# Six rows of 1/rms by way of memory in place of products with the identity

## The chip, the cores and the metric

The kernel runs on one core of one Trainium2 chip. The metric is the device time of an execution in microseconds, the median of several runs.

## The reference

One layer of a bidirectional hybrid encoder over 512 tokens of width 1024, all in float32. What matters here is the RMS normalisation, which occurs six times in the part that is changed:

```
def rms_norm(x, g):
    y = xf * lax.rsqrt(jnp.mean(xf * xf, axis=-1, keepdims=True) + EPS)
    return (y * g).astype(x.dtype)

def gated_group_rmsnorm(y, z, g):           # four groups of 512 columns
    v = (y * silu(z)).reshape(bsz, s, SSD_GROUPS, d // SSD_GROUPS)
    v = v * lax.rsqrt(jnp.mean(v * v, axis=-1, keepdims=True) + EPS)
```

The layer normalises x, makes one wide input projection, runs a state space branch (SSD: a convolution, two chunked scans, a gated RMS norm in four groups, a projection) and a branch of windowed attention, merges both by sigmoid gates, projects and adds to x; then cross-attention into 256 normalised memory tokens (its queries come from rms_norm(x)), then a SwiGLU FFN (its input is rms_norm(x)), then a last rms_norm.

## The kernel before, in words

Activations lie transposed: 128 features on the partitions, 512 tokens along the free axis. Each product runs in three matmuls per 128 x 128 weight block, on a high and a low part of both operands (`mac`, L134 to L141); a projection (`proj`) has 24 of them and gathers its result in one PSUM bank. The banks have three tags: "mm" (three banks, for projections), "sa" (two) and "sb" (three, for small things).

A normalisation's factor 1/rms depends on the token alone, so the kernel applies it after the projection: the projection runs on x times the gain, and its result is multiplied by a row that holds 1/rms of each token, the same on all partitions. Three steps make that row. A sum of squares by token is gathered while x is produced. `rms_stat` (L149 to L167) sums it over the partitions by matmuls against a column of ones, which leaves a token on each partition and a column for each of the four chunks of 128 tokens, and takes the power -0.5 on GpSimd (POOL, L161) with one refining step on VectorE (L163 to L166); its result r is 128 x 4. `rms_row` (L176) then turns r into the row: `rms_bank` (L169) multiplies, for each chunk, a column of r spread over 128 columns with the identity (L172), which puts the row on all partitions of an "sb" bank, and ScalarE copies it to SBUF (L178).

Rows made so, apart from those of the first stage and of the end: `vrow` for each of the four scan groups (`group_row`), `row1` in the cross-attention (`xa_row`) and `row2` in the FFN (`ff_row`). Their readers:

- `group_out` (L636): eight results of an out projection are multiplied by `vrow` on VectorE (L644 in the first group, L647 in the others) and added to the branch's sum on POOL (L648). Each result holds an "mm" bank until its product with the row.
- `xq_out` (L943): VectorE multiplies a q result by `row1` (L949), ScalarE and VectorE split it into a high and a low part (L950, L951); the scores (`xattend`, L966) of a head need two such tiles.
- `ff_act` (L1044): VectorE multiplies a gate result by `row2` (L1048), ScalarE takes SiLU, POOL multiplies by the row again (L1050), VectorE by the up result (L1052).

The program is a list of steps, which names the weights that each step needs; weights are loaded two steps ahead by the sync engine's queue and split by ScalarE (L129) and VectorE (L130). Up to the step `cutat`, which lies behind the last scan group, the steps stand in a block whose order on each engine a planner works out from its own estimates of durations (`tc.block(schedule_with_timeline_sim=True)`); the later steps are ordered by the default planning. In either case each engine runs its instructions in the order planned. In the scan, POOL weights the inputs (L495), masks the decay rows (L537) and adds the two directions (L550); VectorE multiplies that sum (L555) before TensorE uses it (L565). In the steps list of a group, the statistics and the row of the group before are woven into the first half of the scan; for the last group they stand at the end of the scan, followed by `group_out(3)`. The gates of the branch (`early_gate`, L653 to L659) are further projections near the end of the scan whose results ScalarE empties.

Of the kernel before, what the change touches and what calls it, by code (L numbers as in the profile page):

```python
# [9 lines left out]
F32 = mybir.dt.float32  # L10
# [5 lines left out]
P = 128  # L16
D = 1024
S = 512
KT = D // P
NCH = S // P  # L20
# [52 lines left out]
def bidir_hybrid_layer(ctx: ExitStack, tc: tile.TileContext, io, dbg=None):  # L73
    nc = tc.nc
# [9 lines left out]
    dram = ctx.enter_context(tc.tile_pool(name="dram", bufs=1, space=bass.MemoryType.DRAM))  # L84
# [9 lines left out]
    def bank(tag):  # L94
        return ps.tile([P, 512], F32, tag=tag, name=tag, bufs={"mm": 3, "sa": 2, "sb": 3}[tag])
# [73 lines left out]
    def rms_bank(r, nchunk):  # L169
        rb = bank("sb")  # L170
        for c in range(nchunk):
            nc.tensor.matmul(rb[:, c * P:(c + 1) * P], r[:, c:c + 1].broadcast_to([P, P]), ident,  # L172
                             start=True, stop=True)
        return rb

    def rms_row(pool, r, nchunk, tag, bufs=1):  # L176
        row = pool.tile([P, S], F32, tag=tag, name=tag, bufs=bufs)[:, :nchunk * P]
        nc.scalar.copy(row, rms_bank(r, nchunk)[:, :nchunk * P])  # L178
        return row

    def add_square(pool, acc, t, first, n, eng, tag="sq", bufs=1):
# [15 lines left out]
    st = {}  # L197
# [56 lines left out]
    def mem_row():  # L254
        st["mrow"] = rms_row(st["sp"], st["mr"], 2, "sq", 1)
# [52 lines left out]
    def x_row():  # L308
        st["xrow"] = rms_row(st["sp"], st["xr1"], NCH, "vrow")
# [356 lines left out]
        st["vr"] = rms_stat(st["sp"], st["vsq"], NCH, S, 4.0 * EPS)  # L666

    def group_row():
        st["vrow"] = rms_row(st["sp"], st["vr"], NCH, "vrow")

    add(ssd_open)
    first, last = group_in(0)
# [2 lines left out]
    for g in range(G):  # L675
        z, (more, turn) = group_z(g), group_in(g + 1) if g + 1 < G else ([], [])
        scan1, scan2 = group_scan(g)
        out = group_out(g - 1) if g else kv[KV1:]
        early = [(early_gate(m), (full(io["w_in"][G_GS + m]),)) for m in range(4)] if g == G - 1 else []
        kinds = {"m": list(more), "z": z[ZP:], "o": list(out), "e": early,  # L680
                 "r": [(group_rms, ())] if g else [], "w": [(group_row, ())] if g else []}

        def take(order):
            return [kinds[c].pop(0) for c in order if kinds[c]]

        one = take(ONE if g < G - 1 else ONE + "e")
        if g == 0:
            one += take("o" * len(kinds["o"]))
        two = take(TWO if g < G - 1 else LAST)
        steps += z[:ZP] + last  # L690
        steps += weave(scan1, one)
        steps += weave(scan2, two)
        last = turn
    add(group_rms)
    add(group_row)
    steps += group_out(G - 1)
    add(apply_early)
# [235 lines left out]
        st["xr2"] = rms_stat(st["xa"], st["acc1"], NCH, D, EPS)  # L933

    def xa_row():
        st["row1"] = rms_row(st["xa"], st["xr2"], NCH, "row1")

    def xq_step(m):
        def f(w):
# [72 lines left out]
    add(xa_rms)  # L1012
    steps += xq[1:2]
    add(xa_row)
    for h in range(4):
        if h < 3:
# [17 lines left out]
        st["xr3"] = rms_stat(st["ff"], st["acc2"], NCH, D, EPS)  # L1034

    def ff_row():
        st["row2"] = rms_row(st["ff"], st["xr3"], NCH, "row2")

    def ff_in(i):
        def f(w):  # L1040
# [72 lines left out]
    for j in range(FKT):  # L1113
        add(ff_in(2 * j), full(io["w_fi"][2 * j]))
        if j == 0:
            add(ff_rms)
        add(ff_in(2 * j + 1), full(io["w_fi"][2 * j + 1]))
        if j == 0:
            add(ff_row)
        add(ff_act(j))  # L1120
# [120 lines left out]
```

## Time and profile before

| | |
|---|---|
| median of 3 runs | 1302.97 us (1302.38 to 1303.30) |
| profiled execution | 1303.36 us, its span 1301.6 us |
| TensorE (PE) busy | 1253.2 us, 96% of the span |
| VectorE (DVE) busy | 773.0 us, 59% |
| ScalarE (ACT) busy | 565.5 us, 43% |
| GpSimd (POOL) busy | 290.7 us, 22% |
| granted TensorE clock | 0.991 of 2.4 GHz |

Times in the rows are microseconds from the span's start. An engine's busy time adds up its instructions; the bracket behind an instruction says how long its engine had been idle before it and which instruction ended the idle time.

### The profile page before, as it was taken

The page shows a single profiled execution, that of the slowest core. Times are in us where ns is not written, and L with a number is a line of the kernel's source. Part 1 is how long each engine was busy: PE and PEld are TensorE (multiplying, and loading weights), DVE is VectorE, ACT ScalarE, POOL GpSimd, SP SyncE. Part 2 cuts the span into 40 slices and gives each one's busy share as a digit, 9 for nine tenths or more (in the row PEclk, how much of TensorE's full clock was granted, in tenths as well). Part 3 has the DMA queues.
Part 4 walks back from the last instruction along what each step waited for, and adds up shares of the span by engine and source line. Part 5 has one row for each costly group of instructions (what it writes and reads, how often), then busy time and mean ns, then how long its engine had stood idle before and what let it go on. Part 6 is the DMA issues. An engine that isn't in the chain of part 4 may idle for free.

```text
span 1301.6 us, 16248 instructions
## 1 busy us (share of the span) xinstructions
PE 1253.2 (96%) x6076; PEld 1011.6 (78%) x6076; DVE 773.0 (59%) x1235; ACT 565.5 (43%) x1062; POOL 290.7 (22%) x250
## 2 busy tenths in 40 slices
PE   7998899999989999999999999999999999999996
PEld 5776588778678688877667888887888888888886
DVE  6785896687777865678873445665444444432323
ACT  6557645365455232358783234444332222222220
POOL 2004722442571733111000002001111111110001
PEclk9999899999999999999999999999999999999998
DMA  7446553454354232321114333322322223233331
GB/s 252 153 138 179 160 166 122 130 157 135 108 152 131 85 120 69 120 98 33 49 34 145 97 99 104 123 65 65 97 94 97 96 94 95 97 97 96 92 98 65
DMA packets 49614, 143.48 MB, mean 110 GB/s; under 512 B 5120, under 2 KB 8576, under 8 KB 49536
## 3 DMA queue, kind: packets, MB, share of 16 engines
q1 hardware_dynamic: 47536, 138.58, 34.5%
q0 software_dynamic: 704, 2.10, 0.4%
q10 hardware_dynamic: 1296, 1.77, 0.4%
q8 instruction: 48, 0.79, 0.3%
q14 instruction: 30, 0.25, 0.1%
HBM read 137.97 MB, written 4.46 MB: 109 GB/s over the span
## 4 chain that ended last, share of the span: by engine, by line
PE 59%; issue 5%; DVE 2%; ACT 2%; POOL 1%; DMA 0%; DVEq 0%; ACTq 0%; POOLq 0%
PE mm L139 18%; PE mm L141 18%; PE mm L140 18%; PE sb L823 1%; PE sb L810 1%; PE sb L997 1%; PE sa L966 1%; POOL rsw L722 1%; PE sa L782 1%; ACT rsw L721 0%; ACT whi L129 0%; PE sa L784 0%; ACT sm L795 0%; PE sb L154 0%; PE sb L172 0%
## 5 line engine op out<-in xcount | busy, mean ns | idle before, releaser
L129 ACT CAST whi<-raw 128x1024 fp32r<-128x1024 f32 (+2 forms) x192 | 199.0, 1036 | 467.6 <-PE mm L140 390.7
L139 PE MATMUL mm<-hh,whi 128*128 128x512 f32 x968 | 382.5, 396 | 5.6 <-DVE cvu L414 2.2
L141 PE MATMUL mm<-hh,wlo 128*128 128x512 f32 x968 | 380.5, 393 | 0.9 <-DVE wlo L130 0.9
L140 PE MATMUL mm<-hl,whi 128*128 128x512 f32 x968 | 380.0, 393 | 0.0
L130 DVE TENSOR_TENSOR wlo<-raw,whi 128x1024 fp32r<-128x1024 f32 (+2 forms) x202 | 250.3, 1239 | 153.8 <-ACT whi L129 144.1
L139 PEld LDWEIGHTS mm<-hh,whi 128*128 128x128 f32 x968 | 182.7, 189 | 47.0 <-issue 5.7
L141 PEld LDWEIGHTS mm<-hh,wlo 128*128 128x128 f32 x968 | 182.6, 189 | 40.2 <-issue 1.8
L140 PEld LDWEIGHTS mm<-hl,whi 128*128 128x128 f32 x968 | 182.8, 189 | 36.8 <-issue 1.0
L544 ACT ACTIVATE rt<-rt,nb 128x128 f32<-128x128 f32 x256 | 78.4, 389 | 61.7 <-POOL rt L537 61.7
L187 POOL TENSOR_TENSOR sq_acc<-sq_acc,sq 128x512 f32<-128x512 f32 x14 | 24.3, 1738 | 262.9 <-ACT sq L186 262.9
L1050 POOL TENSOR_TENSOR fa<-fa,row 128x512 f32<-128x512 f32 x22 | 39.0, 1775 | 192.4 <-ACT fa L1049 192.4
L139 PE MATMUL mm<-vh,whi 128*128 128x512 f32 (+1 forms) x192 | 71.1, 371 | 9.2 <-DVE cvu L414 5.6
L139 PE MATMUL mm<-fh,whi 128*128 128x512 f32 (+1 forms) x198 | 72.6, 367 | 0.0
L140 PE MATMUL mm<-fl,whi 128*128 128x512 f32 (+1 forms) x198 | 72.4, 365 | 0.0
L141 PE MATMUL mm<-fh,wlo 128*128 128x512 f32 (+1 forms) x198 | 72.3, 365 | 0.0
L414 DVE SCALAR_TENSOR_TENSOR cvu<-mm,hcw,cvu 128x510 f32<-128x510 f32 (+1 forms) x96 | 71.1, 743 | 1.3
L141 PE MATMUL mm<-vh,wlo 128*128 128x512 f32 (+1 forms) x192 | 70.5, 367 | 0.0
L140 PE MATMUL mm<-vl,whi 128*128 128x512 f32 (+1 forms) x192 | 68.4, 356 | 0.0
L537 POOL TENSOR_SCALAR_AFFINE_SELECT rt<-rt 128x512 f32<-128x512 f32 x64 | 48.0, 776 | 57.4 <-DMA rt<-adr 55.5
L1052 DVE TENSOR_TENSOR ft<-fa,mm 128x512 f32<-128x512 f32 x22 | 15.1, 688 | 72.9 <-PE mm L141 70.7
L550 POOL TENSOR_TENSOR mt<-rt 128x512 f32<-128x512 f32 x32 | 46.1, 1454 | 19.8 <-PE sa L565 19.8
L139 PEld LDWEIGHTS mm<-vh,whi 128*128 128x128 f32 x192 | 36.6, 190 | 17.8 <-issue 7.3
(230 smaller groups left out, 1941.0 us busy)
## 6 DMA issues: line engine op xcount, KB each, us to landing
raw<-in_w_in SPq DMA_DIRECT2D x69, 512.0 KB, 3.5
raw<-in_w_fi SPq DMA_DIRECT2D x44, 512.0 KB, 3.5
rt<-adr SPq DMA_DIRECT2D x32, 512.0 KB, 5.5
ear<-edr SPq DMA_DIRECT2D x32, 256.0 KB, 4.4
raw<-in_w_bs SPq DMA_DIRECT2D x16, 512.0 KB, 3.5
raw<-in_w_fo SPq DMA_DIRECT2D x16, 512.0 KB, 3.5
raw<-in_w_xk SPq DMA_DIRECT2D x8, 512.0 KB, 3.5
raw<-in_w_ba SPq DMA_DIRECT2D x8, 512.0 KB, 3.5
```

What stands on the lines that cost most here:

```text
L129: nc.scalar.copy(hi[:, t], raw[:, t])
L130: (nc.gpsimd if i in LO_POOL else nc.vector).tensor_tensor(lo[:, t], raw[:, t], hi[:, t].bitcast(F32), op=ALU.subtract)
L139: nc.tensor.matmul(acc, wh, xh[:, k0 + k], start=first and k == 0, stop=False)
L140: nc.tensor.matmul(acc, wh, xl[:, k0 + k], start=False, stop=False)
L141: nc.tensor.matmul(acc, wl, xh[:, k0 + k], start=False, stop=last and k == nk - 1)
L187: eng.tensor_tensor(acc, acc, sq, op=ALU.add)
L414: nc.vector.scalar_tensor_tensor(u[:, b], acc[:, a], w5[j], u[:, b], op0=ALU.mult, op1=ALU.add)
L537: nc.gpsimd.affine_select(out=rt[:, d].rearrange("p (c l) -> p c l", c=NCH), in_=rt[:, d].rearrange("p (c l) -> p c l", c=NCH), pattern=[[ ...
L544: nc.scalar.activation(r, r, AF.Exp, bias=st["nb"][:, c, e0:e0 + 1])
L550: nc.gpsimd.tensor_tensor(mt, st["rt", g, h][:, 0], st["rt", g, h][:, 1], op=ALU.add)
L1050: nc.gpsimd.tensor_tensor(a, a, st["row2"], op=ALU.mult)
L1052: nc.vector.tensor_tensor(t, a, st["fp", 2 * j + 1], op=ALU.mult)
```

## The change

The six rows named above go another way. r (128 x 4, a token on each partition) is written to a small tensor in memory in the order of the tokens, by a DMA that POOL issues; a second DMA, also issued by POOL, reads these 512 numbers back as a row for each of the 128 partitions. The products with the identity and the copy by ScalarE go. The first stage's rows and the last normalisation keep the old way.

```diff
     def rms_row(pool, r, nchunk, tag, bufs=1):
         row = pool.tile([P, S], F32, tag=tag, name=tag, bufs=bufs)[:, :nchunk * P]
         nc.scalar.copy(row, rms_bank(r, nchunk)[:, :nchunk * P])
+        return row
+
+
+    def rms_sent(pool, r, tag):
+        rdr = dram.tile([1, S], F32, tag="rdr", name="rdr", bufs=2)
+        nc.gpsimd.dma_start(rdr.rearrange("o (c p) -> p (o c)", p=P), r)
+        row = pool.tile([P, S], F32, tag=tag, name=tag, bufs=1)
+        nc.gpsimd.dma_start(row, rdr.broadcast_to([P, S]))
         return row
...
     def group_row():
-        st["vrow"] = rms_row(st["sp"], st["vr"], NCH, "vrow")
+        st["vrow"] = rms_sent(st["sp"], st["vr"], "vrow")
...
     def xa_row():
-        st["row1"] = rms_row(st["xa"], st["xr2"], NCH, "row1")
+        st["row1"] = rms_sent(st["xa"], st["xr2"], "row1")
...
     def ff_row():
-        st["row2"] = rms_row(st["ff"], st["xr3"], NCH, "row2")
+        st["row2"] = rms_sent(st["ff"], st["xr3"], "row2")
```

## Rows read from the trace of the kernel before

**Rows 1.** Busy time of each engine by stage: us, then each engine, clock, DMA.

```profile
core 0: us, PE busy (x) PEld busy (x) DVE busy (x) ACT busy (x) POOL busy (x), PEclk, DMA share, GB/s
...
395.00:495.00 100.00, 97.76 (x495) 77.26 (x494) 73.34 (x91) 36.63 (x62) 39.62 (x30) 1.00 0.37 111
495.00:538.00 43.00, 41.49 (x190) 34.08 (x189) 24.21 (x33) 7.39 (x10) 12.88 (x9) 1.00 0.28 91
...
926.00:1162.00 236.00, 236.00 (x1051) 195.64 (x1050) 96.89 (x115) 71.53 (x90) 38.28 (x22) 1.00 0.30 96
```

**Rows 2.** The chain that ended last, around the last group's row: start, us, what.

```profile
505.27 0.91 PE sb L172 x8
506.20 0.59 ACT vrow L178
506.82 0.70 DVE cvt L647
507.57 0.50 PE mm L139
```

**Rows 3.** Timeline, last scan group: r's last step, and the matmul that waited.

```profile
504.13 0.16 DVE L166 SCALAR_TENSOR_TENSOR rms_r<-rms_t,rms_r 128x4 f32<-128x4 f32 x1
...
507.57 0.50 PE L139 MATMUL mm<-vh,whi 128*128 128x512 f32 x1 [1.40 <-DVE cvt L647]
```

**Rows 4.** Timeline, cross-attention, from r to the first scores and the turn.

```profile
818.83 0.16 DVE L166 SCALAR_TENSOR_TENSOR rms_r<-rms_t,rms_r 128x4 f32<-128x4 f32 x1
...
821.02 0.59 ACT L178 COPY row<-sb 128x512 f32<-128x512 f32 x1
...
825.60 0.69 DVE L951 TENSOR_TENSOR ql<-qf,qh 128x512 fp32r<-128x512 f32 x1 [0.69 <-ACT qh L950]
...
826.30 0.28 PE L966 MATMUL sa<-kvh,qh 128*128 128x256 f32 x1
...
834.73 1.03 PE L986 MATMUL sb<-cst,pe 128*128 128x128 f32 x8
```

**Rows 5.** Timeline, FFN: r, its row, and the starts of two products.

```profile
934.17 0.16 DVE L166 SCALAR_TENSOR_TENSOR rms_r<-rms_t,rms_r 128x4 f32<-128x4 f32 x1
...
938.84 0.59 ACT L178 COPY row<-sb 128x512 f32<-128x512 f32 x1
...
944.12 0.39 PE L139 MATMUL mm<-hh,whi 128*128 128x512 f32 x1
...
949.56 0.39 PE L139 MATMUL mm<-hh,whi 128*128 128x512 f32 x1
```

**Rows 6.** Timeline, first and third scan group: r, POOL's work, the row.

```profile
228.24 0.16 DVE L166 SCALAR_TENSOR_TENSOR rms_r<-rms_t,rms_r 128x4 f32<-128x4 f32 x1
...
231.30 1.04 POOL L495 TENSOR_TENSOR xw<-xk,wt 128x512 f32<-128x512 f32 x1 [0.82 <-PE sb L503]
...
238.33 0.59 ACT L178 COPY vrow<-sb 128x512 f32<-128x512 f32 x1 [1.04 <-PE sb L172]
...
238.74 2.52 POOL L550 TENSOR_TENSOR mt<-rt 128x512 f32<-128x512 f32 x2 [6.39 <-PE sa L565]
...
426.06 0.16 DVE L166 SCALAR_TENSOR_TENSOR rms_r<-rms_t,rms_r 128x4 f32<-128x4 f32 x1
...
434.55 0.59 ACT L178 COPY vrow<-sb 128x512 f32<-128x512 f32 x1 [3.31 <-PE sb L172]
```

**Rows 7.** DMA issues: queue, count, KB each, median us from issue to landing.

```profile
rt<-adr SPq DMA_DIRECT2D x32, 512.0 KB, 5.5
ear<-edr SPq DMA_DIRECT2D x32, 256.0 KB, 4.4
...
out_t<-x ACTq DMA_DIRECT2D x8, 128.0 KB, 1.9
```

**Rows 8.** POOL's stores of 128 KB: ns min/median/max on POOL, us to landing.

```profile
L262 POOL DMA_DIRECT2D kdr<-xw x8: 539/557/598, 48.2 to 172.3; - x8
...
DMA to landing us min/median/max: 2.2/2.6/9.5
```

## The prediction

> **What bounds the kernel now.** I read the busy time by stage first: TensorE (PE) is busy 98% in the stretch that holds the third scan group's row, 96% in the one that holds the last group's and 100% in the FFN's first half, with the clock granted in full [rows 1]. No other engine is near that. So what takes an instruction off PE is a gain where PE never waits, and what makes PE wait is a loss of the same size, with no later idle time to win it back from: the stages behind are as full.
>
> Next I read the chain that ended last around the last group's row. It runs through the very thing that is changed: the products with the identity (0.91 us), the copy by ScalarE, VectorE's product with the row (L647), and only then the next matmul [rows 2]. PE stands there because a result tile can be emptied only once the row is known, and all three "mm" banks hold such results. The timeline gives the times: r, the four columns of 1/rms, is ready at 504.13 + 0.16 = 504.29, the row at 506.20 + 0.59 = 506.79, and PE goes on at 507.57, released by L647 [rows 2, 3]. From r to row it is 2.5 us, and from row to the next matmul 0.78.
>
> I then looked at the five other rows for the same two times. In xa, r is ready at 818.99, the row at 821.61, and the first score product, which needs two q tiles made from the row, starts at 826.30 [rows 4]. In ff, r is ready at 934.33 and the row at 939.43; the product that needs a freed bank starts at 944.12, and such a product takes 949.56 - 944.12 = 5.44 us [rows 5]. In the first scan group r is ready at 228.40 and the row at 238.92; the second group repeats this 100 us later; in the third it is 426.22 and 435.14 [rows 6]. So the time that each row may take before it is later than today is 10.5, 10.5, 8.9, 2.5, 2.6 and 5.1 us.
>
> **What the change removes.** Six times four products (eight matmul instructions): 0.9 us of PE each, 5.4 in all, by the 0.91 of the chain [rows 2]. Six copies of 0.59 us on ScalarE, which is no bound anywhere, and one "sb" bank for their length: nothing.
>
> **What it adds: the trip.** Each row becomes a store by token, issued on POOL's queue, and a load of 2 KB to each of 128 partitions, also on POOL's queue, which can't be issued before the store has landed. Call T the time from r to the row in SBUF; it is serial. No row shows a store of 512 pieces of 4 bytes. The nearest from below is a 128 KB output store, 1.9 us [rows 7]; POOL's own stores of 128 KB take 2.2 at least, 2.6 at the median, 9.5 at most, and POOL is held 0.56 us for the issue [rows 8]. Those have 128 pieces of the same kind; 512 pieces could cost up to 3 x 0.56 = 1.7 us more to issue. I take 3.2: the median 2.6 plus a third of that. The load is nearest to the broadcast ear<-edr, also 256 KB of 2 KB rows from memory, 4.4; the larger broadcast takes 5.5, and at the bottom a load as quick as POOL's 128 KB store would take 2.6 [rows 7, 8]. I take 4.4. With 0.2 for the two handovers (my estimate) T = 7.8. The ends are 1.9 + 2.6 = 4.5 and 9.5 + 5.5 = 15; the upper one needs the worst of eight stores every time, so I carry 12.
>
> The rows put POOL's store at 2.6 us at the median and POOL's hold at 0.56 [rows 8]. The Trainium skill (DMA: Bandwidth & Descriptors, "Anatomy of one DMA — SWDGE (gpsimd) path") gives a gpsimd transfer about 2.0 us fixed plus its bytes over 436 GB/s. By it, as an estimate, the trip would be 2.0 and 2.6 us, 4.6 in all, and the sum below would come out near no change; the fastest POOL store, 2.2 us, agrees with it, the median does not quite. The same page ("Rules for kernel authors") says that a last dimension that isn't contiguous becomes one descriptor per element, which speaks against this store; no row here shows what that costs.
>
> **The terms, as they follow from T.**
>
> Last scan group: PE goes on at 504.29 + T + 0.78 instead of 507.57, so the change is T - 2.5, which already contains the removed 0.9. At 7.8: +5.3. Nothing hides it: all three banks wait for the row, every later product needs a bank, and POOL, idle here, adds nothing.
>
> xa: with 0.9 us less PE work the third q product ends at 826.30 - 0.9 = 825.4 and fills the last bank. A bank comes free at 818.99 + T + 0.78 = 827.6. If the next q product goes first, PE is 827.6 - 826.3 = 1.3 later than today. If the scores must go first, they come 4.69 us behind the row (826.30 - 821.61 today), at 831.5: +5.2. The fourth q product (5.44 us) stands behind the scores today, and used up early it no longer covers the softmax before the turn at 834.73 [rows 4]. I take +2.5, nearer to the low end, since products with hh already lie between the scores.
>
> ff: a bank is free at 934.33 + T + 0.78 = 942.9, and PE, 0.9 us ahead, wants it at 943.2. Hidden: -0.9. Without that cover (T over 8.1) it grows with T; at T = 9 it is zero.
>
> First three scan groups: T fits into 10.5, 10.5 and 8.9, so -0.9 each, -2.7 in all, if the store goes out at once. But POOL's queue is in order: if the store stands behind the two weighting products (L495), the second of which ends at 231.30 + 1.04 = 232.34, the row arrives at 240.1, 1.2 us late, and with the 0.9 that is +0.3 each, +0.9 in all. Behind the load's wait stand POOL's sums mt (L550), which VectorE and then PE need; POOL has 6.39 us idle before them in the first group, which covers it [rows 6]. I take the middle of -2.7 and +0.9: -0.9.
>
> Sum: +5.3 + 2.5 - 0.9 - 0.9 = +6.0. The profiled execution took 1303.36 (span 1301.6 and 1.8 around it), 0.39 above the median of the runs, 1302.97; so 1309.4 against the one and 1309.0 against the other.
>
> **The rivals.**
>
> Dear trip: the 512 pieces cost what they might, T = 12. Last group +9.5; xa 819.8 + 12 - 826.3 = +5.5; ff 935.1 + 12 - 944.1 = +3.0; scan groups 1.5 + 1.5 + 3.1 late less 2.7, +3.4. Sum +21.4: 1324. For it: nothing in the trace is as scattered. Against: only 2 KB move.
>
> Cheap trip, T = 4.5: -2.7 + 2.0 - 0.9 - 0.9 = -2.5: 1300.5. For it: the output stores at 1.9. Against: both broadcasts in the trace are over 4. The Trainium skill's rule above (4.6 us) leads here.
>
> Cover at the last group, the other side: the order inside the scan block comes from a planner, which will now see a long wait there. If it puts one of the last gate products (L657; its bank is emptied by ScalarE without the row) behind the statistics, PE has 5.44 us of work for a wait of 5.3, and the last group gains 0.9 instead of losing 5.3. With the scan rows hidden: -2.7 - 0.9 + 1.3 - 0.9 = -3.2: 1299.8. It decides as long as T is under 7.9. Against: a planner that takes what is ready first has no reason to keep a gate product back.
>
> POOL held: in the scan groups the load's wait for the store (3.2 us) stops L495 and L550 behind it, and PE waits for them. At full price 3 x 3.2 - 2.7 = +6.9 in place of -0.9: sum +13.8, 1316.8. For it: POOL is the in-order queue of the masks and sums. Against: the idle 6.39.
>
> **How the numbers follow.** Forecast 0.50 (its own range 1304.5 to 1314, T from 7 to 10 and xa from 1.3 to 5.2); dear trip 0.17; cheap trip 0.12; cover 0.10; POOL held 0.11. The range 1300 to 1322 takes in the cheap trip and POOL held, and leaves out most of the dear trip and part of the cover. 0.2% is 2.6 us, about what a measurement here can tell from no change: faster is below 1300.4, slower above 1305.6. Faster: 0.07 of the cover and 0.04 of the cheap trip, 0.11. Same: the rest of both, 0.11, and 0.08 of the forecast, 0.19. Slower: 0.70.
>
> **What would show it.** In the changed kernel's timeline: PE idle of about 8 us behind the last group's statistics, released by L647's counterpart; xa with PE idle about 2 us before the fourth q product; ff without idle; the store's landing near 3.2 us and the load's near 4.4. PE's busy time should be about 5 us less. The prediction is wrong if the store's issue holds POOL for several us, if the last group's wait is filled, or if the scan stages, planned anew, move by more than 3 us for reasons that have nothing to do with the rows.

## The result and the profile after

The changed kernel takes 1352.99 us (median of 4 runs, 1351.67 to 1354.36) against 1303.13 of the kernel before, run beside it: 1.0381 of it, 95% interval 1.0368 to 1.0394. That is 50 us slower, where 6 were forecast, and outside the range. The profiled execution took 1354.25 us, its span 1352.3, the mean granted clock 0.970 where before it was 0.991. Behind the row's helper line numbers are 8 higher than before: the store is L184, the load L186, `xw` L503, `group_out` L652 and L655, `xattend` L974.

First the two transfers, all six of each, by their lines: how long POOL was held for the issue, and the time to landing.

```profile
L184 POOL DMA_DIRECT2D rdr<-rms_r x6: 811/833/836, 230.0 to 976.9; - x6
...
DMA to landing us min/median/max: 8.7/9.9/10.2
```

```profile
L186 POOL DMA_DIRECT2D vrow<-rdr x4: 560/578/601, 240.3 to 532.4; - x4
...
L186 POOL DMA_DIRECT2D row<-rdr x2: 560/560/560, 861.3 to 987.0; - x2
...
DMA to landing us min/median/max: 4.0/4.1/4.6
```

The load is what the nearest broadcast had promised (4.4 taken, 4.1 measured). The store of 2 KB is not: 9.9 us at the median where I took 3.2, above the 9.5 of the slowest 128 KB store of [rows 8]. The timeline of the last group shows the whole trip.

```profile
522.71 0.16 DVE L166 SCALAR_TENSOR_TENSOR rms_r<-rms_t,rms_r 128x4 f32<-128x4 f32 x1
...
523.17 0.83 POOL L184 DMA_DIRECT2D rdr<-rms_r  x1 [1.11 <-DVE rms_r L166]
532.44 0.56 POOL L186 DMA_DIRECT2D vrow<-rdr  x1 [8.44 <-DMA rdr<-rms_r]
536.43 0.69 DVE L655 TENSOR_TENSOR cvt<-mm,vrow 128x512 f32<-128x512 f32 x1 [13.56 <-DMA vrow<-rdr]
...
537.18 0.79 PE L139 MATMUL mm<-vh,whi 128*128 128x512 f32 x1 [13.33 <-DVE cvt L655]
...
537.77 0.63 PE L140 MATMUL mm<-vl,whi 128*128 128x512 f32 x1
...
538.20 0.63 PE L141 MATMUL mm<-vh,wlo 128*128 128x512 f32 x1
```

r is ready at 522.87 and its first reader starts at 536.43: T = 13.56 us where [rows 2, 3] had 2.5. In xa T is 865.43 - 851.08 = 14.35, in ff 991.55 - 976.58 = 14.97, in the three scan groups 14.8 to 14.9.

What the DMA engines did meanwhile stands in the same trace. The next two rows have the form of [rows 1]: a stretch and its length, each engine's busy time, then the clock, the share of time in which the core's 16 DMA engines were busy, and GB/s.

```profile
523.10:525.90 2.80, 0.75 (x4) 0.29 (x2) 0.00 (x0) 0.00 (x0) 0.83 (x1) 1.00 0.53 188
525.90:532.40 6.50, 0.00 (x0) 0.00 (x0) 0.00 (x0) 0.00 (x0) 0.00 (x0) 0.75 0.00 0
```

The store's packets lie in the first stretch and end 2.7 us behind its issue. From then to the load's issue at 532.44 the trace has no packet on any DMA engine. So by these records the landing, 8.7 us behind the issue, waited neither for pieces that were still being sent nor for other traffic; what passes in these 6 us the trace doesn't show.

PE's waits, added up by what ended them (us, times, longest), are now headed by the readers of the row and, in first place, by POOL's weighting products:

```profile
PE sb L511 <- POOL xw L503: 15.6, 5, 5.5
PE mm L139 <- DVE cvt L655: 14.6, 4, 13.3
PE sa L974 <- ACT qh L958: 9.4, 1, 9.4
...
PE mm L139 <- DVE fa L1056: 6.8, 1, 6.8
```

In the kernel before the same four entries are 2.3, 3.8, none and none. Where the 50 us lie is read from busy time by stage, cut in both kernels at the first matmul of each row's statistics: the three scan groups with a row inside, the stretch from the last group's statistics to xa's, from xa's to ff's, and from ff's to the end's. Kernel before:

```profile
224.40:324.50 100.10, 98.94 (x505) 78.90 (x504) 75.31 (x104) 51.98 (x112) 38.55 (x36) 1.00 0.47 137
324.50:421.80 97.30, 90.08 (x470) 72.09 (x468) 75.86 (x98) 49.27 (x107) 47.12 (x41) 1.00 0.46 130
421.80:501.20 79.40, 77.97 (x396) 60.91 (x396) 53.92 (x65) 25.39 (x44) 38.27 (x29) 1.00 0.32 100
501.20:813.50 312.30, 307.95 (x1450) 240.10 (x1449) 194.34 (x443) 157.98 (x330) 35.90 (x24) 1.00 0.26 84
813.50:931.40 117.90, 117.29 (x579) 96.88 (x578) 70.83 (x127) 51.98 (x94) 11.16 (x6) 1.00 0.27 88
931.40:1279.80 348.40, 348.40 (x1578) 290.07 (x1577) 129.81 (x149) 97.23 (x118) 48.07 (x30) 1.00 0.30 93
```

Changed kernel:

```profile
225.70:331.10 105.40, 100.77 (x499) 79.28 (x497) 74.81 (x104) 51.35 (x111) 39.07 (x38) 0.97 0.54 133
331.10:433.00 101.90, 93.21 (x454) 72.81 (x453) 73.18 (x95) 47.86 (x105) 50.95 (x43) 0.95 0.48 122
433.00:519.80 86.80, 79.92 (x397) 61.77 (x396) 54.34 (x68) 25.51 (x45) 39.36 (x31) 0.96 0.35 100
519.80:845.40 325.60, 309.44 (x1443) 241.15 (x1442) 193.26 (x443) 157.13 (x329) 37.78 (x26) 0.98 0.25 82
845.40:973.60 128.20, 118.52 (x570) 97.20 (x569) 70.61 (x127) 51.68 (x93) 12.58 (x8) 0.96 0.26 82
973.60:1330.20 356.60, 349.78 (x1569) 290.59 (x1568) 129.68 (x149) 96.78 (x117) 48.90 (x32) 0.99 0.31 91
```

The first two numbers of a row are the stage's length and PE's busy time; their difference is PE idle. The six stages are longer by 5.3, 4.6, 7.4, 13.3, 10.3 and 8.2, together 49.1 us. Idle time rose by 3.5, 1.5, 5.4, 11.8, 9.1 and 6.8: 38.1. The other 11.0 are busy time, which should have fallen by 5.4. So the remaining products took 16.4 us longer, and the clock column says how: 1.00 in each stage before, 0.95 to 0.99 now. It is low in the stretches that hold the late waits and what follows them:

```profile
519.80:554.00 34.20, 20.87 (x85) 16.83 (x84) 12.46 (x19) 3.15 (x3) 12.83 (x10) 0.80 0.18 51
845.40:880.00 34.60, 25.15 (x120) 20.41 (x119) 15.68 (x32) 11.37 (x20) 3.35 (x3) 0.85 0.37 106
973.60:1010.00 36.40, 29.58 (x126) 24.11 (x125) 11.24 (x17) 9.45 (x11) 7.01 (x6) 0.91 0.42 73
```

In the timeline above the first matmul behind the wait of 13.33 us takes 0.79 us; behind the 1.40 us wait of [rows 3] it took 0.50. The mean of such a stretch mixes two levels. This one lies inside the first and is at 0.50 throughout, 1.2 GHz; it began while PE waited:

```profile
529.15:542.80 13.65, 5.62 (x13) 4.46 (x14) 3.27 (x5) 0.48 (x1) 4.54 (x4) 0.50 0.13 19
```

In the six stages there are seven stretches at 0.50, four of them in the scan, and PE is busy for 32 us in them. A matmul starts 0.43 us after the one before there (537.77 to 538.20), against 5.44 / 24 = 0.23 in full clock [rows 5]. By that, as an estimate, some 15 of the 16.4 us are the clock. So the account is 38.1 of idle, less 5.4 of products taken away, plus 16.4 of slower products, 9.6 of them in the scan groups.

### The profile page after: what moved, and what is told of

It is laid out like the page before. It is cut to its first block, busy times and chain, and to the rows that moved or that the text cites. A ratio compares the mean times of both kernels' runs of the same rounds, so it can differ in the third digit from the quotient of the medians.

```text
span 1352.3 us, 16158 instructions
## 1 busy us (share of the span) xinstructions
PE 1264.8 (94%) x6028; PEld 1016.6 (75%) x6028; DVE 769.0 (57%) x1235; ACT 562.2 (42%) x1056; POOL 300.6 (22%) x262
## 4 chain that ended last, share of the span: by engine, by line
PE 64%; DMA 12%; issue 8%; DVE 6%; POOL 6%; ACT 4%; SPq 0%; ACTq 0%; POOLq 0%; DVEq 0%
PE mm L139 19%; PE mm L140 19%; PE mm L141 19%; DMA rt<-adr 4%; DMA rdr<-rms_r 4%; DVE wlo L130 2%; POOL mt L558 2%; ACT whi L129 1%; POOL rt L545 1%; DVE cvu L422 1%; PE sb L831 1%; DMA vrow<-rdr 1%; ACT rt L552 1%; PE sb L818 1%; PE sa L974 1%
## 5 line engine op out<-in xcount | busy, mean ns | idle before, releaser
L139 PE MATMUL mm<-vh,whi 128*128 128x512 f32 (+1 forms) x192 | 75.3, 392 | 21.4 <-DVE cvt L655 14.4
L140 PE MATMUL mm<-vl,whi 128*128 128x512 f32 (+1 forms) x192 | 72.9, 380 | 0.0
L139 PEld LDWEIGHTS mm<-vh,whi 128*128 128x128 f32 x192 | 39.6, 206 | 31.1 <-DVE cvt L655 16.4
L1056 DVE TENSOR_TENSOR fa<-mm,row 128x512 f32<-128x512 f32 x22 | 15.2, 691 | 67.9 <-PE mm L141 54.1
```

The lines of the kernel that those rows point to most:

```text
L139: nc.tensor.matmul(acc, wh, xh[:, k0 + k], start=first and k == 0, stop=False)
L140: nc.tensor.matmul(acc, wh, xl[:, k0 + k], start=False, stop=False)
L1056: nc.vector.tensor_tensor(a, st["fp", 2 * j], st["row2"], op=ALU.mult)
```

## The experiments

Ratios are against the kernel before, run on the same chip beside each; its medians lay between 1303.1 and 1304.1.

**Why is the store slow?** Three kernels add stores, for which nobody waits, to the kernel before, at the FFN's output products; each kind runs three times. `e_micro`:

```diff
+        if k == 0:
+            nc.gpsimd.dma_start(pdr[0].rearrange("o (c p) -> p (o c)", p=P), ptmp[:, 0:4])
+        elif k == 1:
+            nc.gpsimd.dma_start(pdr[1].rearrange("o (p c) -> p (o c)", p=P), ptmp[:, 0:4])
+        elif k == 2:
+            nc.gpsimd.dma_start(pdr[2].rearrange("o (p c) -> p (o c)", p=P), ptmp[:, 0:1])
+        elif k == 3:
+            nc.gpsimd.dma_start(pdr[3].rearrange("(c p) w -> p c w", p=P)[:, :, 0:1],
+                                ptmp[:, 0:4].rearrange("p (c w) -> p c w", w=1))
...
```

> The kernel before, with 21 extra stores to scratch memory from the FFN's stages, three of each of seven shapes; nobody waits for them, so the time should stay within 2 us of 1303. Read is the time from issue to landing. Theory A (each small piece is written to memory for itself, one after the other on its DMA engine): 512 pieces of 4 B as in the change 9.9 us; 128 pieces of 16 B and 128 pieces of 4 B about 4; 512 pieces of 4 B, each 512 B from the next, 9.9; 512 pieces of 64 B 9.9; from ScalarE's queue 9 to 10. Rival B (the pieces disturb each other because neighbours of one line come from several DMA engines): the spread pieces 3 to 4, the 128 pieces of 4 B still near 9. Rival C (it is POOL's way of issuing that is slow): from ScalarE's queue 2 to 3.

`e_pitch` varies the distance of 512 pieces of 4 bytes:

```diff
+    pitch = (2, 4, 8, 16, 32, 64)
+    pdr = [dram.tile([S, w], F32, tag=f"pdr{w}", name=f"pdr{w}") for w in pitch] + [
...
+        dst = pdr[k].rearrange("(c p) w -> p c w", p=P)[:, :, 0:1] if k < 6 else None
```

> The kernel before with 21 extra stores from POOL that nobody waits for, three of each shape: 512 pieces of 4 B, each 8, 16, 32, 64, 128 or 256 B from the next, and 128 pieces of 32 B side by side. Theory B (pieces that share a line are written one after the other, some 0.4 us each): the time from issue to landing falls as fewer pieces share a line: if the line has 64 B, about 6 us at 8 B (8 pieces share one), 4 to 5 at 16 B, 3 to 4 at 32 B, 3.0 to 3.6 from 64 B on; if it has 512 B or more, still over 5 us at 64 B. Pieces of 32 B side by side: 3 to 4. Rival A (the number of pieces): near 10 for all six pitches.

`e_dense` varies how many pieces lie side by side, and how long they are:

```diff
+    shape = ((P, 4, 1), (P, 4, 2), (P, 4, 4), (P, 2, 1), (P // 2, 4, 1), (P // 8, 4, 1))
...
+            dst = pdr[k].rearrange("c p w -> p c w")
+            src = ptmp[0:p, 0:c * w].rearrange("p (c w) -> p c w", w=w)
```

> The kernel before with 21 extra stores on POOL's queue, three of each of seven kinds, which nobody waits for; the landing of each kind is read. Neighbouring pieces written at once by different engines of the DMA share a line of memory and wait for each other (theory): 512 pieces of 4 bytes side by side 10 us again, 512 of 8 bytes side by side half to three quarters of that, 512 of 16 bytes 4 to 5, 256 of 4 bytes 8 to 9, 64 partitions of 4 pieces about 9, 16 partitions of 4 pieces 5 or less, 128 pieces of 4 bytes at a pitch of 8 about 4. Rival (the delay is a fixed one of any store with pieces of 4 bytes that lie side by side, not one that adds up along a line): all kinds with 4-byte pieces side by side take the same 8 to 10, 16 partitions too, and 8-byte pieces 4 or less.

The three took 1302.46, 1304.11 and 1303.80 (one run each), so the stores cost nothing there that can be seen. Median landing in us; all from POOL's queue but the one marked:

| pieces | side by side | landing |
|---|---|---|
| 512 x 4 B, as in the change | yes | 10.2 (`e_micro`), 9.4 (`e_dense`) |
| the same from ScalarE's queue | yes | 9.8 |
| 256, 256 (64 partitions), 128, 64 x 4 B | yes | 9.5, 8.5, 8.4, 6.6 |
| 512 x 8 B, 512 x 16 B | yes | 5.2, 3.0 |
| 128 x 16 B, 128 x 32 B | yes | 4.6, 1.7 |
| 512 x 4 B at a pitch of 8, 16, 32, 64, 128, 256 B | no | 4.0, 3.3, 2.6, 2.6, 2.7, 2.5 |
| 512 x 4 B at a pitch of 512 B | no | 3.6 |
| 128 x 4 B at a pitch of 8 B | no | 4.7 |
| 512 x 64 B, 512 x 512 B | no | 3.8, 3.0 |

Two rows of `e_micro`, by their lines, are the heart of it: the same 512 pieces of 4 bytes, the first side by side, the second 512 bytes apart.

```profile
L119 POOL DMA_DIRECT2D pdr<-ptmp x3: 793/793/845, 943.3 to 1091.8; - x3
...
DMA to landing us min/median/max: 9.6/10.2/10.6
```

```profile
L125 POOL DMA_DIRECT2D pdr<-ptmp x3: 798/798/798, 972.1 to 1124.4; - x3
...
DMA to landing us min/median/max: 3.0/3.6/4.2
```

The landings of one kind differ: 128 pieces of 16 bytes took 4.6 us here and 1.8 in `e_store16` below. POOL issues both of the kinds shown in 0.8 us, so theory A (the number of pieces) and rival C (POOL's issuing) fall, and what rival B forecast came: the price is pieces of 4 bytes that lie side by side. In `e_pitch` the landing falls with the distance as forecast, but at each distance it is below the forecast. In `e_dense` 64 neighbours already take 6.6, against my 5 or less, and 512 take no longer than 256; so the delay doesn't add up along the row as the theory of `e_dense` had it, nor is it the same for all, as its rival had it. By which mechanism they hinder each other, and whether it takes several DMA engines as rival B has it, stays open.

**What does each part cost?** Two kernels send only some of the rows by memory, the others by products. `e_scan3` the first three scan rows:

```diff
-        st["vrow"] = rms_sent(st["sp"], st["vr"], "vrow")
+        st["rows"] = st.get("rows", 0) + 1
+        st["vrow"] = (rms_sent(st["sp"], st["vr"], "vrow") if st["rows"] < 4
+                      else rms_row(st["sp"], st["vr"], NCH, "vrow"))
...
-        st["row1"] = rms_sent(st["xa"], st["xr2"], "row1")
+        st["row1"] = rms_row(st["xa"], st["xr2"], NCH, "row1")
...
-        st["row2"] = rms_sent(st["ff"], st["xr3"], "row2")
+        st["row2"] = rms_row(st["ff"], st["xr3"], NCH, "row2")
```

> Only the rows of the first three scan groups go by way of memory, the three later ones as before. By the changed kernel's stages these three cost 5.3 + 4.7 + 7.3 = 17.3 us: 1320, if the rows' costs simply add up. Rival (the stages move for the planner's reasons, and the rows' own price in the scan is small): under 1310.

1320.19, ratio 1.0122 (1.0099 to 1.0146), as the stages said. `e_last1` sends the last group's row alone (`== 4` in place of `< 4`):

> Only the last scan group's row goes by way of memory. By the changed kernel's stages 13.3 us: 1316. My formula with the measured trip of 14.5 us gives 12.0 without the clock. Rival (the order planned anew fills the wait when it is the only one): under 1308.

1316.88, ratio 1.0100 (1.0078 to 1.0123), as the stages said; PE stands 13.55 us. So the scan, which the forecast counted as a small gain, costs more than the last group: 16 us against 13.

**Is it the store?** `e_store16` keeps all six trips but writes r as 128 pieces of 16 bytes, a partition's four tokens together; the row comes back in that order and its readers step through it by 4:

```diff
-        nc.gpsimd.dma_start(rdr.rearrange("o (c p) -> p (o c)", p=P), r)
+        nc.gpsimd.dma_start(rdr.rearrange("o (p c) -> p (o c)", p=P), r)
...
-        return row
+        return row.rearrange("q (p c) -> q c p", p=P)
+
+    def by4(ap):
+        return ap.rearrange("q (c p) -> q c p", p=P)
...
-                        nc.vector.tensor_tensor(t, acc, st["vrow"], op=ALU.mult)
+                        nc.vector.tensor_tensor(by4(t), by4(acc), st["vrow"], op=ALU.mult)
```

> All six rows by way of memory, but the store writes the four numbers of a partition together (128 pieces of 16 B), and the readers take the row through a view with a step of four. Theory A: the store lands in about 4 us, the trip is about 8.5, and the time falls to 1309 to 1316. Rivals B and C: the store stays at 8 us or more and the time above 1340. If the view with a step of four is dear on VectorE or POOL, L1056 and L1058 take longer than 0.69 and 1.78 us.

1313.15, ratio 1.0072 (1.0047 to 1.0096): 40 of the 50 us are gone. The store lands in 1.8 us at the median (1.7 to 3.9), T is 7.07 in the last group, 8.97 in xa and 6.8 to 7.2 elsewhere. This is about the kernel that my forecast described, T near 7.8. The run alone would fit theory A too, as it has fewer pieces; `e_micro` and `e_pitch` decide between them. Its last three stages, cut as above:

```profile
499.40:819.20 319.80, 309.66 (x1444) 241.27 (x1442) 196.25 (x443) 157.12 (x329) 37.59 (x26) 0.98 0.26 83
819.20:943.90 124.70, 119.97 (x570) 98.00 (x569) 73.45 (x127) 51.79 (x93) 12.35 (x8) 0.97 0.27 85
943.90:1291.40 347.50, 347.50 (x1570) 289.20 (x1569) 136.49 (x149) 98.34 (x117) 48.09 (x32) 1.00 0.30 93
```

The last group's stage is 7.5 longer than before (idle +5.8, busy +1.7), xa's 6.8 (idle +4.1, busy +2.7), ff's 0.9 shorter. The three scan groups (98.4, 94.6 and 79.8) are 4.0 shorter together. The product with the stepped row takes VectorE 1.08 us, against the 0.70 of [rows 2].

`e_scan3_16` sends only the first three scan rows so:

> Only the rows of the first three scan groups by way of memory, stored in pieces of 16 B; the later rows as before. With the trip at about 7 us these three rows are hidden behind slacks of 8.9 to 10.5 us, and 2.7 us of TensorE's work is gone: 1300 to 1302 against 1303. Rival (VectorE's dearer view, 24 reads at 1.08 us instead of 0.68, or POOL's hold costs the scan more than that): 1305 to 1310.

1298.86 (10 runs), ratio 0.9966 (0.9953 to 0.9978): faster than both kernels, and below the 1300 to 1302 expected. In the profiled execution the three scan groups make 3.6 us of the gain (273.2 against 276.8). `e_scan3_ff_16` sends ff's row too:

> First three scan rows and the FFN's row by memory with the 16-byte store, the last group's and the cross-attention's rows by products as in the kernel before. Theory (the FFN's row hides a trip of about 7 us, and the removed 0.9 us of PE is a gain): 1298, 0.9 less than with the three scan rows alone (1298.86), that is 0.995 of the kernel before. Rival (the products with the row on a view of step 4 cost VectorE and POOL more than PE gains): 1299.5 or more.

1300.18 (9 runs), ratio 0.9967 (0.9955 to 0.9980). ff's stage is 347.5 against 348.4 in both `e_scan3_16` and the kernel before, the 0.9 foreseen. The first stage, with the same instructions in the same order, was 2.7 longer in its profiled execution (209.3 against 206.6 from its own statistics to the first scan row's), so executions differ by more than the 0.9, and the whole gained nothing that can be seen.

**In the scan: POOL held, or the row late?** `e_split` is `e_scan3` with the load as a later step of its own:

```diff
-ONE = "mrwomomoo"
+ONE = "mrwmlomooo"
...
+    def group_fetch():
+        st["vrow"] = rms_fetch(st["sp"], st["rdr"], "vrow")
```

> The first three scan rows go by memory with the store as in the change; only the load is a later step of the block, so that POOL's weighting products need not stand behind its wait for the store. Theory (two costs in the scan: POOL held by the load's wait, and the row late): the gaps ahead of L503's matmuls, 15.6 us in all for the kernel whose load follows its store directly (1320.19), fall to 4 or less, and a part of them comes back as a wait for the row itself, since the store still lands after about 10 us: 1308 to 1314. Rival (the row being late is all that counts, POOL's hold only shows the same delay at another place): the gaps move to the matmuls that need an emptied bank and the time stays at 1318 or above.

1320.17, ratio 1.0131 (1.0107 to 1.0154). It tells nothing: in the first two groups the planned order left one weighting product ahead of the load and the next behind it, as before, POOL stood 24.7 us before it as against 25.8, and the gaps before L503's readers were 18.8. Two more kernels take the causes apart. `e_hold3` makes all rows by products and has the trip for nothing beside them:

```diff
+    def rms_sent(pool, r, tag):
+        rdr = dram.tile([1, S], F32, tag="rdr", name="rdr", bufs=2)
+        nc.gpsimd.dma_start(rdr.rearrange("o (c p) -> p (o c)", p=P), r)
+        row = pool.tile([P, P], F32, tag=tag, name=tag, bufs=1)
+        nc.gpsimd.dma_start(row, rdr[:, 0:P].broadcast_to([P, P]))
+        return row
...
+        if st["rows"] < 4:
+            rms_sent(st["sp"], st["vr"], "vtwin")
```

> The kernel before, all rows made by products with the identity; in the first three scan groups POOL also stores r by 512 pieces of 4 bytes side by side and then loads 128 of these numbers into a tile that nobody reads. So POOL stands before the load for the store's 10 us as in the change, but no row is late. Theory H (in the scan the cost is POOL's queue standing still ahead of the weighting products): PE waits for L495 some 15 us in all and the kernel takes 1316 to 1320, as with the three rows really sent (1320.19). Theory L (the cost is the row, late by 3 to 5 us a group): 1304 to 1307, within 0.2% of the kernel before. Something between measures the share.

1325.42, ratio 1.0160 (1.0140 to 1.0180). Its timeline on POOL, first group: the load `vtwin`, which no one reads, keeps the last weighting product from 232.4 to 241.1.

```profile
230.50 0.84 POOL L184 DMA_DIRECT2D rdr<-rms_r  x1 [0.89 <-DVE rms_r L166]
231.37 1.06 POOL L503 TENSOR_TENSOR xw<-xk,wt 128x512 f32<-128x512 f32 x1
240.52 0.60 POOL L186 DMA_DIRECT2D vtwin<-rdr  x1 [8.09 <-DMA rdr<-rms_r]
241.14 1.06 POOL L503 TENSOR_TENSOR xw<-xk,wt 128x512 f32<-128x512 f32 x1
```

```profile
PE sb L511 <- POOL xw L503: 15.6, 5, 6.0
```

`e_scan3_sync` issues the load of `e_scan3` from SyncE's queue:

```diff
-        nc.gpsimd.dma_start(row, rdr.broadcast_to([P, S]))
+        nc.sync.dma_start(row, rdr.broadcast_to([P, S]))
```

> First three scan rows by memory with the store as in the change, the load issued from SyncE's queue, so that POOL doesn't stand for the store; the row is as late as before, and what stands behind the load is now SyncE's queue, the weights two steps ahead and the decay rows. Theory H (POOL's queue is the cost): no gap ahead of the weighting products' readers, 1304 to 1310. Theory L (the late row): 1317 or above, with PE waiting for emptied banks. If SyncE's standing still costs as POOL's does, PE waits for weights (whi, wlo) or decay rows instead, and the time says nothing for H or L.

1326.29, ratio 1.0170 (1.0149 to 1.0190). PE's waits and VectorE's timeline in the first group:

```profile
PE mm L139 <- DVE cvt L655: 15.9, 4, 9.0
...
PE mm L139 <- DVE x L652: 5.5, 1, 5.5
PE sb L511 <- POOL xw L503: 3.2, 2, 2.6
```

```profile
232.45 0.91 DVE L516 TENSOR_TENSOR hin<-hin,dec 128x512 f32<-128x512 f32 x1
243.99 1.29 DVE L652 TENSOR_TENSOR x<-mm,vrow 128x512 f32<-128x512 f32 x2 [10.62 <-DMA vrow<-rdr]
...
246.32 0.68 DVE L518 TENSOR_TENSOR hin<-hin,sb 128x512 f32<-128x512 f32 x1
```

Each cause alone costs at least what both cost together: over the three groups, cut as above, `e_hold3` has 11.1 us more idle than the kernel before, `e_scan3_sync` 15.4, the changed kernel 10.4 and `e_scan3` 8.9. As a whole, too, both take longer than `e_scan3`, and `e_hold3` longer than theory H had it; 2.7 us of that are products with the identity that it keeps. So the two costs lie side by side in time and don't add up. Without POOL's wait the gap before L503's readers falls to 3.2, and VectorE, which stands 10.62 us before the row's first reader with the state's updates (L518) queued behind it, holds PE instead. The weights and the decay rows, whose loads stand on SyncE's queue too, did not: PE's wait for weights is 7.1, before 6.9, and that for the scan's `mt`, made from the decay rows, 2.8, before 5.6.

**The late waits.** `e_last1_cover` is `e_last1` with the last two gate products put behind the row's step:

```diff
-LAST = "zezee"
+LAST = "zez"
...
+    steps += early
```

> Only the last scan group's row by way of memory with pieces of 4 B (1316.9 so far), but the last two gate products stand behind the row's step. If nothing but uncovered waiting costs the last group 13 us, the 10.9 us of gate products fill most of it: 1304 to 1308. Rival (the gate products were needed where they stood, as filling in the scan): 1312 or more.

1312.52, ratio 1.0069 (1.0051 to 1.0087): PE stands 8.38 us in place of 13.55. The gate products didn't go into the wait (ScalarE empties the last of them at 500.0, before the row's store at 501.9). What moved is the statistics: 9.7 us of PE's work stand from their start to the wait, where `e_last1` has 4.1. The time is where the rival put it; its reason isn't shown. `e_xa_order` is `e_store16` with the fourth q product ahead of the first scores:

```diff
-        steps += xq[2 * h + 2:2 * h + 3] + [(xattend(h), ())] + xq[2 * h + 3:2 * h + 4] + [(xmix(h), ())]
+        k = 4 if h == 0 else 2 * h + 3
+        steps += xq[2 * h + 2:k] + [(xattend(h), ())] + xq[k:2 * h + 4] + [(xmix(h), ())]
```

> All six rows by memory with the 16-byte store (1313.15), and in the cross-attention the fourth q product is put ahead of the first head's scores in the steps. Theory (the change's planned order took the dear end of the term of the cross-attention, scores ahead of the fourth product, for which PE stood 4.4 us): PE waits only for a bank, and the kernel takes 1309, about 4 less. Rival (the product moved forward leaves the same gap at the softmax later on): no change, 1313.

1312.47, ratio 1.0068 (1.0051 to 1.0086), no difference that can be told: PE waits 3.15 for a bank in place of 4.40 for the scores, and the granted clock is as low (0.86 in the stage's first 24.7 us, 0.87 in the other's first 25.9). The order was not what made xa dear.

`e_warm` fills the three late waits of the changed kernel with products that nobody reads, to tell the wait from the clock behind it:

```diff
+    def keep_warm(n):
...
+            for i in range(n):
+                nc.tensor.matmul(acc, st["hh"][:, i % KT, 0:P], st["hh"][:, i % KT], start=i == 0, stop=i == n - 1)
...
+    steps += out[:1] + [(keep_warm(44), ())] + out[1:]
```

> The changed kernel with products whose results nobody reads in the three late waits: 44 behind the last group's first out step, 36 before the first scores, 28 in the FFN before its fourth product. Theory: the granted clock no longer falls to 1.2 GHz there, and the 1 to 3 us that each of the three waits cost beyond its length come back: 1345 to 1350 against 1353. Rival (the clock's fall costs nothing, the losses are the waits alone): 1353 or, where the products last longer than the wait, more.

1351.46, ratio 1.0368 (1.0343 to 1.0394), against 1.0381 without fillers: missed, and as a whole no difference that can be told. Only ff's wait was filled nearly whole; there the clock stayed at 1.00, and the stage took 354.6 in place of 356.6:

```profile
976.30:1012.70 36.40, 35.98 (x163) 29.60 (x162) 12.06 (x19) 10.55 (x13) 7.01 (x6) 1.00 0.45 80
```

So about 2 us of ff's 8.2 come back with the clock. That fits the rows at 0.50: ff has 4.4 us of busy time in them in the changed kernel and none here. At the last group 3.9 us of idle stayed and the clock fell there; in xa PE stood five more times for q tiles and the softmax behind the fillers, 0.2 to 1.15 us each, and the clock fell there (0.89 from 870 to 900). Both stages came out no shorter than without fillers (326.4 and 132.4, against 325.6 and 128.2). What the clock alone costs there is not shown by an experiment, only by the account of busy time and of the rows at 0.50 above.

## Why the prediction was wrong, step by step

**The failed step is the term of the store.** I took 3.2 for it and 7.8 for T; the store measured 9.9 and T 13.6 to 15.0. The stores of [rows 8] that I took it from have 128 pieces too, but of 1 KB each, so "of the same kind" was wrong. I sized the scatter by the issue, as up to 1.7 us for more pieces, but the issue grew only from 0.56 [rows 8] to 0.83 us, and the landing by 7. The dear trip was the rival that came true, with T near its upper end of 15. That end held by luck: the store passed its 9.5, and the load stayed below its 5.5. I carried T = 12 against the 15 that the rows allowed, because "only 2 KB move", and the bytes were no measure. The Trainium skill (DMA: Bandwidth & Descriptors, "Rules for kernel authors") warned against it with its descriptor per element; the number of pieces is yet not the price, as 512 of them at a pitch of 32 bytes land in 2.6 us. The Trainium skill (DMA: Bandwidth & Descriptors, "Specifications") gives 512 bytes as the least transfer for full rate, with a read-modify-write below it. That rule has a size and no distance, and the 512 pieces of 4 bytes in the table above differ by their distance alone, from 2.5 to 10.2 us.

**How each term grows with T was right behind the scan.** Last group: T - 2.5 with T = 13.56 is 11.1, which with the 0.9 of products gone means 12.0 of idle; measured 11.8. ff: hidden up to T = 8.1, so 6.9 of idle at 14.97; measured 6.8, and with the short store of `e_store16` the -0.9 came to the tenth. xa: 2.5 + (14.35 - 7.8) + 0.9 = 10.0; measured 9.1; the 2.5 itself was a choice between 1.3 and 5.2.

**The scan's term was too large with T as measured, and its reason half of the matter.** T less 10.5, 10.5 and 8.9 gives 14.6 of idle, measured 10.4. I had the late row as the forecast and POOL held as a rival to it; the runs show each to be enough by itself. The 6.39 us of POOL's idle time [rows 6], which I put against POOL held, cover its sums and not the weighting product that stands behind the load in the order planned. With a store of 1.8 us neither is left to speak of (1.7 us less idle than before over the three groups of `e_store16`), and the scan gains 4.0 where I took 0.9.

**The clock was missing.** I wrote that a wait of PE is "a loss of the same size", and forecast 5 us less busy time; it is 11.6 more (1264.8 against 1253.2), because the granted clock fell at the waits. Of the 50 us, 16.4 are slower products. With T as measured my terms give 43.5 us of idle less 5.4, 38 in all, against 49 measured in the six stages: the idle came out 5.4 less than that, and the 16.4 stood in no term. In `e_store16`, where T was near the forecast, the stages of the last group and xa cost 7.5 and 6.8 against 5.3 and 2.5: idle time less 0.9 explains 4.9 and 3.2, and the other 2.6 and 3.6 are longer busy time, with 6.2 and 5.7 us of it at 1.2 GHz.

**Of the other rivals,** the cover at the last group didn't come by itself, and the steps of `e_last1_cover` got a part of it, from 1.0100 to 1.0069; the cheap trip needed T = 4.5, and the shortest in these kernels is 6.7.

## What to carry to other kernels

Price a small transfer by the size of its pieces and by what lies next to each, not by its bytes: where no row shows the pattern, carry the upper bound. Writing fewer and longer pieces (128 of 16 bytes here) repaired most of this change, and where the row had about 9 us of slack or more made it a gain. In these runs the trip through memory held both in-order queues on its way, the issuer's at the store's landing and the reader's at the load's; taking the wait off one of them shows the other, so look for both before moving either. And waits of 4 to 13 us on a full TensorE cost more than their length here: add what the products behind them lose to the granted clock.

## What the hardware showed that I had not expected

- A store of 512 pieces of 4 bytes side by side lands in 9.4 to 10.2 us at the median, from POOL's queue or ScalarE's; at a pitch of 8 bytes 4.0, at 32 bytes 2.6. 64 such neighbours take 6.6 us, 128 pieces of 32 bytes side by side 1.7.
- In the last group of the changed kernel the packets of such a store end 2.7 us behind its issue, and it lands 8.7 us behind it, with no packet on any DMA engine between.
- POOL's issue of 512 pieces takes 0.8 us, of 128 pieces 0.6.
- With a wait of 13.3 us in it the granted clock of the stage's first 34.2 us was 0.80, with 9.4 us 0.85 over 34.6, with 6.8 us 0.91 over 36.4; with ff's wait filled it was 1.00 over 36.4.
- VectorE's product of 128 x 512 with a row read at a step of 4 takes 1.08 us, against 0.70 for the plain one.
